# Three places in the instruction order of a two-layer decoder trunk: one copy, two loads and one step of gate arithmetic

## The chip, the core and the metric

The kernel runs on one core of a Trainium2 chip. The metric is the device time of one execution in microseconds (us), and of several runs their median. The core's engines work side by side, each through its own queue in order: TensorE (PE) multiplies matrices, with weight loads as a stream of their own (PEld); VectorE (DVE) and ScalarE (ACT) do elementwise work; SyncE (SP) issues the transfers (DMA) between HBM and the core's memory SBUF. PE writes its sums into PSUM, which here is a pool of eight banks. An engine that needs another's result waits for its semaphore, and everything behind it in its queue waits too.

## The reference, cut to what matters

Input x is 1024 tokens by 1024 numbers, float32. There are two layers, each a token mixer followed by an MLP, with an RMSNorm ahead of each, residual adds, and one RMSNorm at the end.

```
layer 0:  x = x + dilated_attention(rmsnorm(x))       # 3 groups of 8 heads, merged
          x = x + (relu(h @ w_up)**2) @ w_down         # MLP, 1024 -> 4096 -> 1024
layer 1:  q, k, v, g_out, gate_lr = split(h @ w_in)    # gated linear attention, 4 heads
          log_a = log_sigmoid(gate_lr @ w_gate_up + b) / 16
          o = chunked recurrence over (q, k, v, log_a), chunks of 64
          x = x + (rmsnorm(o) * silu(g_out)) @ w_out
          x = x + MLP as above
out = rmsnorm(x)
```

## The kernel before

**Products.** Every float32 operand is split into a rounded high part (made on ACT) and the remainder (made on DVE), and each product is three matmuls: high by high, high by low, low by high. The large products are Strassen-like: seven products (q or s = 0 to 6) of half-size blocks instead of eight, whose sums are formed by ACT copies and DVE adds out of PSUM.

**The first half of each MLP** (class Up, run at L668). It goes through 16 column blocks p, each with seven products s of 12 matmuls (L596). Product s of block p accumulates into bank "XYXVXZV"[s], so bank X takes s = 0, 2 and 4 in turn, and its contents are copied out (L601, tile e) after each of these before the next may write: e1, e2, e3. From p = 4 on (L703) the program issues in each step s: the product, then what `done(p, s - 1)` says of the product before, then `stage(p + 1, s)`, one piece of the weights for the next block (rounding on ACT, L533, remainder on DVE, L534, differences t on DVE, L561 to L571). At s = 2, done is the add c11 (DVE, L633) and its two squares, Relu and Square (ACT, L605 and L606), and a store; at s = 3, done is the copy e2. Product 4 must wait for e2. Rows p = 0 to 3 are written out by hand; p = 4 takes over from them.

**The gated layer's values and output gates** (gla_values, L1718; class Mixed, L872). 28 steps n, 24 matmuls each (L823), in two rounds g: steps 0 to 13 make g_out, steps 14 to 27 make v. Products accumulate into two sets of four banks, A and B. `sums(n)` (L845) copies finished banks on ACT (L890 or L833) and adds others on DVE (L838). `prep(n + 2)` splits the weights two steps ahead (ACT L802, DVE L808 and L778). The 16 finished pieces of g_out then go through the gate, one a step from n = 7 on, in three stages: `begin` (ACT exp, L902), in the next step `guard` (DVE, L907) and `logs` (ACT ln and exp, L912 and L913), in the one after `close` (three DVE instructions, L919 to L921, and a store to ggscr, L922). In step n the order is guard, close, sums, prep, load, product, logs, begin. From step 24 on `W.pump()` also prepares the next stage's weights (ACT L151, DVE L152).

**The heads** (gla_keys, L1935). For each of four heads h and two halves: `start_gates`, then `dense_T` for keys and for queries (24 matmuls each, L213 to L215). Between them, ticks run the previous head's recurrence: pairs of outputs are squared on ACT (L1823), scaled on DVE (L1830) and stored to oscr (L1835). In the last half of the last head, two loads of 512 KB each bring back finished outputs (ahead_k4, L1234, tiles ol), and during the query product `turn(0)` transposes them on PE (L259), which the output projection needs.

**What sets the order.** The order of each engine's queue is the order in which the program issues, written by hand. Tiles come from pools: k4 (25 buffers), t2 (8 buffers, among them c, e, gd, ge and gy), PSUM banks (8). A new tile waits for the last reader of the buffer that it gets. SP issues transfers in order, and a store waits there for its data.

## Time and profile before

| what | value |
|---|---|
| median of 3 runs | 2626.88 us (2626.61 to 2629.28) |
| the profiled execution | 2625.36 us |
| its span, first to last instruction | 2623.6 us |
| PE busy | 2588.1 us, 99% |
| DVE busy, ACT busy | 1860.3 us (71%), 1275.9 us (49%) |
| DMA, share of the 16 engines | 50.3% |
| mean granted clock of PE | 0.999 |

A row of a timeline has the start in us, the time taken in us, the engine, the line, the operation with its output and inputs, and how many were merged (x2). In square brackets stands the idle time of the engine before it and who ended it. A row of the list of waits has the waiting engine and line, what it waited for, and the total, the number and the longest in us. Line numbers are those of the kernel before.

### The profile page before, as it was taken

The page shows a single profiled execution, that of the slowest core. Times are in us where ns is not written, and L with a number is a line of the kernel's source. Part 1 is how long each engine was busy: PE and PEld are TensorE (multiplying, and loading weights), DVE is VectorE, ACT ScalarE, POOL GpSimd, SP SyncE. Part 2 cuts the span into 40 slices and gives each one's busy share as a digit, 9 for nine tenths or more (in the row PEclk, how much of TensorE's full clock was granted, in tenths as well). Part 3 has the DMA queues.
Part 4 walks back from the last instruction along what each step waited for, and adds up shares of the span by engine and source line. Part 5 has one row for each costly group of instructions (what it writes and reads, how often), then busy time and mean ns, then how long its engine had stood idle before and what let it go on. Part 6 is the DMA issues. An engine that isn't in the chain of part 4 may idle for free.

```text
span 2623.6 us, 33036 instructions
## 1 busy us (share of the span) xinstructions
PE 2588.1 (99%) x12144; PEld 2159.7 (82%) x12144; DVE 1860.3 (71%) x2986; ACT 1275.9 (49%) x2319; POOL 1.8 (0%) x7
## 2 busy tenths in 40 slices
PE   8999999999999999999999999999999999999998
PEld 6888888888888888888888887878888888888887
DVE  7645888888888768666657577977658866656666
ACT  6333455556555446555533345654326555553343
POOL 0000000000000000000000000000000000000000
PEclk9999999999999999999999999999999999999999
DMA  5533365655656633454775452462513545395543
GB/s 189 168 129 125 101 162 137 158 155 144 159 144 182 221 121 129 165 169 138 284 249 185 137 191 93 142 188 97 190 55 127 171 141 169 123 353 206 186 147 125
DMA packets 327010, 423.12 MB, mean 161 GB/s; under 512 B 19808, under 2 KB 192224, under 8 KB 326848
## 3 DMA queue, kind: packets, MB, share of 16 engines
q1 hardware_dynamic: 326848, 421.01, 50.3%
q8 instruction: 95, 1.56, 0.2%
q14 instruction: 67, 0.55, 0.1%
HBM read 279.71 MB, written 116.06 MB: 151 GB/s over the span
## 4 chain that ended last, share of the span: by engine, by line
PE 87%; DVE 7%; ACT 2%; issue 1%; DMA 1%; SPq 0%; ACTq 0%; DVEq 0%
PE pX L596 16%; PE pB L1570 13%; PE pV L596 10%; PE pA L1570 10%; PE pB L823 6%; PE pY L596 5%; PE pZ L596 5%; PE pA L823 5%; PE pd L214 3%; PE pd L215 3%; PE pd L213 3%; PE pS L970 2%; PE pO L1011 2%; PE pP L997 1%; PE pT L332 1%
## 5 line engine op out<-in xcount | busy, mean ns | idle before, releaser
L1570 PE MATMUL pB<-dh 128*128 128x512 f32 x512 | 199.7, 390 | 0.0
L1570 PE MATMUL pB<-dh,dl 128*128 128x512 f32 x512 | 199.5, 390 | 0.0
L1570 PE MATMUL pB<-dl,dh 128*128 128x512 f32 x512 | 199.5, 390 | 0.0
L222 DVE TENSOR_TENSOR dl<-sin,dh 128x1024 fp32r<-128x1024 f32 x112 | 136.7, 1220 | 44.8 <-ACT dh L219 44.2
L219 ACT ACTIVATE dh<-sin 128x1024 fp32r<-128x1024 f32 x112 | 117.9, 1052 | 90.1 <-PE pB L1570 32.6
L219 ACT ACTIVATE dh<-kept 128x1024 fp32r<-128x1024 f32 x64 | 67.9, 1061 | 183.6 <-DVE kept L1535 137.8
L596 PE MATMUL pV<-s4h,wd 128*128 128x512 f32 x448 | 151.0, 399 | 0.0
L1570 PE MATMUL pA<-dh 128*128 128x512 f32 x384 | 149.6, 390 | 0.0
L1570 PE MATMUL pA<-dl,dh 128*128 128x512 f32 x384 | 149.6, 390 | 0.0
L1570 PE MATMUL pA<-dh,dl 128*128 128x512 f32 x384 | 149.6, 390 | 0.0
L986 ACT ACTIVATE pt<-pt,orow 128x128 f32<-128x128 f32 (+1 forms) x192 | 84.7, 442 | 95.0 <-DVE orow L984 95.0
L1570 PEld LDWEIGHTS pB<-dh,dl 128*128 128x128 f32 x512 | 96.2, 188 | 19.9
L1570 PEld LDWEIGHTS pB<-dh 128*128 128x128 f32 x512 | 96.2, 188 | 19.8
L1570 PEld LDWEIGHTS pB<-dl,dh 128*128 128x128 f32 x512 | 96.2, 188 | 19.8
L534 DVE TENSOR_TENSOR wal<-raw,wah 128x512 fp32r<-128x512 f32 x112 | 76.2, 687 | 42.7 <-ACT wah L533 42.7
L605 ACT ACTIVATE c<-c 128x512 f32<-128x512 f32 x64 | 40.4, 631 | 125.0 <-DVE c L633 81.2
L596 PEld LDWEIGHTS pV<-s4h,wd 128*128 128x128 f32 x448 | 84.2, 188 | 17.6 <-DVE rb L621 0.3
L534 DVE TENSOR_TENSOR wbl<-t,wbh 128x1024 fp32r<-128x1024 f32 x56 | 68.6, 1226 | 39.0 <-ACT wbh L533 39.0
L222 DVE TENSOR_TENSOR dl<-kept,dh 128x1024 fp32r<-128x1024 f32 x64 | 78.4, 1225 | 24.9 <-ACT dh L219 19.0
L984 DVE CUSTOM_DVE_ANT_0 pt<-pS,masks 128x128 f32<-128x128 f32 (+1 forms) x192 | 58.3, 348 | 52.1 <-PE pS L970 52.1
L596 PE MATMUL pX<-s3h,wgh 128*128 128x512 f32 x224 | 87.8, 392 | 2.3 <-ACT e L601 2.3
L596 PE MATMUL pY<-a12h,wah 128*128 128x512 f32 x224 | 89.6, 400 | 0.0
(336 smaller groups left out, 7374.4 us busy)
## 6 DMA issues: line engine op xcount, KB each, us to landing
sin<-acts SPq DMA_DIRECT2D x112, 512.0 KB, 3.7
raw<-in_mlp_w_up_dram SPq DMA_DIRECT2D x64, 512.0 KB, 5.9
acts<-s SPq DMA_DIRECT2D x64, 512.0 KB, 3.4
raw<-in_mlp_w_down_dram SPq DMA_DIRECT2D x64, 512.0 KB, 4.6
raw<-in_attn_w_in_dram SPq DMA_DIRECT2D x96, 256.0 KB, 4.3
cw<-c SPq DMA_DIRECT2D x192, 128.0 KB, 2.3
acts<-c SPq DMA_DIRECT2D x64, 256.0 KB, 2.2
kept<-in_mlp_w_down_dram SPq DMA_DIRECT2D x32, 512.0 KB, 5.7
```

Source lines behind the costliest of these rows:

```text
L213: pe.matmul(ps, sh, mh, start=start, stop=False)
L214: pe.matmul(ps, sh, ml, start=False, stop=False)
L215: pe.matmul(ps, sl, mh, start=False, stop=stop)
L219: act.activation(hi, src, AF.Copy)
L222: dve.tensor_tensor(lo, src, hi.bitcast(F32), op=OP.subtract)
L534: self.remain(lambda: dve.tensor_tensor(lo, src, hi.bitcast(F32), op=OP.subtract))
L596: pe.matmul(st[b], u[:, k, :], v, start=first and k + n == 0, stop=k == 3 and n == 2, skip_group_check=True)
L823: pe.matmul(self.acc[s][t], a[:, c], b[:, k, :], start=fresh and m + k + v == 0, stop=m == 1 and k == 1 and v == 2, skip_group_check=True)
L970: pe.matmul(ps[:, i, :128 * n], self.qT[:, 128 * b:128 * b + 128], self.kT[:, k0:k0 + 128 * n], start=True, stop=True)
L984: dve.tensor_tensor_reduce(pt[:, i, :128 * n], ps[:, i, :128 * n], masks[:, m0:m0 + 128 * n], -scale, 1e38, op0=OP.add, op1=OP.min, accum_ ...
L986: act.activation(pt[:, i, :128 * n], pt[:, i, :128 * n], AF.Exp, scale=-1.0, bias=m, accum_out=self.row[:, r, HD:HD + 1])
L1570: pe.matmul(self.acc[s][t], a[:, k, c], b[:, k, :], start=fresh and m + k + v == 0, stop=m == 7 and k == 1 and v == 2, skip_group_check=True)
```

## The change

Three edits, each to the order in which work is issued. No instruction is added or taken away, and PE's queue is the same as before.

1. In the first half of both MLPs, at p = 4: the two squares of c11 and their store move from step 2 to step 3, behind the copy e2. The add c11 stays. On ACT's queue the order "square, square, copy" becomes "copy, square, square"; nothing else moves.
2. In the gated values, step 13 leaves out guard, close, logs and begin. The ten pieces that begin at step 13 or later run one step later. On DVE, four instructions leave step 13, a guard comes into step 24 and the last close into step 25 (between the wlo of the next stage's weights and the adds of that step); on ACT an exp comes into step 23 and ln and exp into step 24; on SP the last store to ggscr comes behind four loads of the next stage's weights.
3. In the last half of the last head, the two loads ol are issued ahead of the key product instead of behind it. On SP they stand behind one store to oscr of that stretch instead of three.

```
@@ Up.run
                     if s == 1:
                         self.sums(p - 1)
                         self.load(p + 2)
-                    if s > 0 and (p, s) != (4, 1):
+                    if (p, s) == (4, 2):
+                        self.add(4, 1)
+                    elif s > 0 and (p, s) != (4, 1):
                         self.done(p, s - 1)
+                    if (p, s) == (4, 3):
+                        self.squared(4, 1)
                     self.stage(p + 1, s)
@@ gla_values
         for n in range(4, m.STEPS):
-            m.guard()
-            m.close()
+            if n != 13:
+                m.guard()
+                m.close()
             m.sums(n)
...
-            m.logs()
-            if n >= 7:
-                m.begin()
+            if n != 13:
+                m.logs()
+                if n >= 7:
+                    m.begin()
             if n + 3 < m.STEPS:
@@ gla_keys
             start_gates(2 * h + half + 1)
+            if h == GH - 1 and half:
+                ol.extend(ahead_k4(p) for p in range(2))
             dense_T(w[0], hT, half, k_done)
             if h == GH - 1 and half:
-                ol.extend(ahead_k4(p) for p in range(2))
                 turn1.append(Turned(ol, xscr))
             dense_T(w[1], hT, half, q_done, half and (lambda: [t.turn(0) for t in turn1]))
```

## The prediction

> **What bounds the kernel now.** I read the page first, then the list of what TensorE (PE) waits for, then the timelines of PE, its weight loads (PEld), ACT, DVE and SP around each wait that an edit can reach.

> ```profile
> span 2623.6 us, 33036 instructions
> PE 2588.1 (99%) x12144; PEld 2159.7 (82%) x12144; DVE 1860.3 (71%) x2986; ACT 1275.9 (49%) x2319; POOL 1.8 (0%) x7
> PEclk9999999999999999999999999999999999999999
> ```

> PE is busy for 99% of the span, at the full granted clock throughout. No edit takes a matmul away, so only PE's idle time can be won: 2623.6 - 2588.1 = 35.5 us. In the list of PE's waits (total, times, longest, in us) four rows matter:

> ```profile
> PE pT L332 <- DVE xn L252: 11.9, 11, 9.2
> PE pX L596 <- ACT e L601: 2.3, 2, 1.1
> PE pT L259 <- DMA ol<-oscr: 2.0, 1, 2.0
> PE pB L823 <- DVE gq L838: 1.2, 1, 1.2
> ```

> The first is mostly the start of the kernel, which no edit touches. The other three, 5.5 us together, are one for each edit: two stops at the copy, one at the loads, one in the gates. The question is how much of each stays away.

> **Edit 1: the copy ahead of two squares, at p = 4 of both MLPs.** Rows of PE, ACT and DVE there, and the same copy one block later:

> ```profile
> 1060.40 0.39 PE L596 MATMUL pV<-s1h,wbl 128*128 128x512 f32 x1
> 1061.92 0.50 PE L596 MATMUL pX<-s3h,wgh 128*128 128x512 f32 x1 [1.13 <-ACT e L601]
> 1064.78 0.39 PE L596 MATMUL pZ<-a22h,wgh 128*128 128x512 f32 x1
> 2092.01 0.50 PE L596 MATMUL pX<-s3h,wgh 128*128 128x512 f32 x1 [1.13 <-ACT e L601]
> 1060.08 0.63 ACT L605 ACTIVATE c<-c 128x512 f32<-128x512 f32 x1 [2.51 <-DVE c L633]
> 1060.75 0.63 ACT L606 ACTIVATE c<-c 128x512 f32<-128x512 f32 x1
> 1061.29 0.58 ACT L601 ACTIVATE e<-pX 128x512 f32<-128x512 f32 x1
> 1061.76 1.05 ACT L533 ACTIVATE wbh<-t 128x1024 fp32r<-128x1024 f32 x1
> 1060.68 0.69 DVE L562 TENSOR_TENSOR t<-raw,t 128x512 f32<-128x512 f32 x1
> 1064.59 0.69 DVE L571 TENSOR_TENSOR t<-raw,t 128x512 f32<-128x512 f32 x1
> 1065.47 1.05 ACT L533 ACTIVATE wgh<-t 128x1024 fp32r<-128x1024 f32 x1
> 1079.97 0.58 ACT L601 ACTIVATE e<-pX 128x512 f32<-128x512 f32 x1
> 1080.87 0.19 PEld L596 LDWEIGHTS pX<-s3h,wgh 128*128 128x128 f32 x1
> 1670.81 0.39 PE L823 MATMUL pB<-dh,a12h 128*128 128x512 f32 x1
> 1671.94 0.39 PE L823 MATMUL pB<-dh,a12l 128*128 128x512 f32 x1
> ```

> The last two rows give the pace of PE: five steps in 1.13 us, 0.227 us a matmul (the bracket's idle time is taken from modelled ends, so I count starts). Without the stop, the first pX matmul would start at 1060.40 + 0.23 = 1060.63, and pZ twelve matmuls later at 1063.35. It starts at 1064.78: one stop costs 1.43 us. Its cause is plain: the two squares wait for DVE, and the copy, whose PSUM bank was complete when PE left product 2, stands behind them. Put ahead, it is done before PE asks. The squares lose nothing: they still start at 1060.08, when DVE has made c; so does the store behind them.

> What is late next? With the copy gone from there, ACT can round wbh when t (L562) is there, 1060.68 + 0.69 + 0.03 = 1061.40, which is 0.36 us sooner. DVE's next pieces follow wbh, so L571 ends at 1064.59 - 0.36 + 0.69 = 1064.92, and wgh starts at 1064.94 instead of 1065.47: 0.53 us sooner. From wgh to the copy of the next block I find ACT and DVE handing on to each other (wgl, rb, its squares, wd, c12, its squares, wah, the sums, c11, its squares), never waiting for PE. So that copy, still behind its squares at p = 5, moves from 1079.97 by 0.53 only and ends at 1079.44 + 0.58 = 1080.02. PE, 1.43 us ahead, wants the weight load of 1080.87 at 1079.44. It goes at about 1080.06: 0.81 us are kept of it, about 0.85 with the faster restart. After that the chain starts from PE's own pX again and is as far ahead as PE. **Kept: 0.85 us, twice: 1.7 us.** Bounds: nothing of it (0) and all of it (2.9); I take the value at which the rows arrive.

> **Edit 2: step 13 of the gated values without gate arithmetic.** Step 14's product waits at its third bank, which DVE's adds of step 13 must free; they stand behind a guard and three close instructions:

> ```profile
> 1673.52 0.50 PE L823 MATMUL pB<-dh,a12h 128*128 128x512 f32 x1 [1.19 <-DVE gq L838]
> 1683.22 0.39 PE L823 MATMUL pA<-dh,a11h 128*128 128x512 f32 x1
> 1670.38 0.43 DVE L907 TENSOR_SCALAR gd<-gd 128x512 f32<-128x512 f32 x1 [0.48 <-ACT gd L902]
> 1670.73 0.68 DVE L919 TENSOR_TENSOR gd<-gd,ge 128x512 f32<-128x512 f32 x1
> 1672.78 1.28 DVE L838 TENSOR_TENSOR gq<-pA,gq 128x512 f32<-128x512 f32 x2
> 1670.26 1.07 ACT L890 ACTIVATE gq<-pA 128x512 f32<-128x512 f32 x2
> 1671.21 1.06 ACT L802 ACTIVATE dh<-raw 128x1024 fp32r<-128x1024 f32 x1
> ```

> Product 14 has 48 matmuls up to the first pA: 1670.81 + 48 x 0.2267 = 1681.69, but pA starts at 1683.22. The stop costs 1.53 us. Without the four instructions the adds wait for ACT's two copies of the same banks only: the first is done near 1670.85, so the adds run from 1670.9 to 1672.1, and PE wants the bank at 1672.17. The stop goes.

> The ten items still to begin then run one step later, each with its exponentials on ACT and its store on SP. DVE's adds come 1.9 us sooner (1672.78 to 1670.9); its next instruction waits for the rounding that ACT ends at 1671.21 + 1.06 = 1672.27, which leaves 1.7. DVE has no idle time from there to step 24, so it stays 1.7 ahead. The bill comes at steps 24 and 25, where no gate work stood before: a guard (0.35) in 24, and three instructions (1672.78 - 1670.73 = 2.05 us) in 25, behind the wlo of the next stage and ahead of the adds that free two banks:

> ```profile
> 1734.29 1.06 ACT L151 ACTIVATE whi<-raw 128x1024 fp32r<-128x1024 f32 x1 [1.28 <-DMA raw<-in_gla_w_in_dram]
> 1735.38 1.23 DVE L152 TENSOR_TENSOR wlo<-raw,whi 128x1024 fp32r<-128x1024 f32 x1 [3.13 <-ACT whi L151]
> 1736.53 0.68 DVE L838 TENSOR_TENSOR c<-pB,c 128x512 f32<-128x512 f32 x1
> 1738.75 0.19 PEld L823 LDWEIGHTS pB<-dh,a22h 128*128 128x128 f32 x1
> ```

> That wlo waits for a load that SP issues behind stores of step 24, so it comes 1.7 - 0.35 = 1.35 us sooner, not 1.53. The first add then ends at 1736.53 + 0.68 - 1.35 + 2.05 = 1737.91, and PE wants it for the weight load of 1738.75 - 1.53 = 1737.22: a new stop of 0.69 us. **Kept: 1.53 - 0.69 = 0.84 us.** Bounds: -0.5 (the load comes no sooner at all, and the new stop is 2.05) and 1.53 (it comes 2.05 sooner, and there is none). I take the value by the stores, which tie the load to DVE. The store that is moved behind four loads on SP is read only by the load of gG in the heads, much later.

> **Edit 3: two loads ahead of a product.** SP, PE, ACT, the landing times of these loads, and DVE:

> ```profile
> 1868.25 14.73 SPq L1835 DMA_DIRECT2D oscr<-gy  x3
> 1883.07 0.96 SPq L1234 DMA_DIRECT2D ol<-oscr  x2
> 1884.72 0.40 PE L215 MATMUL pd<-a22h,wlo 128*128 128x512 f32 x1
> 1887.11 1.09 PE L259 MATMUL pT<-ident,ol 128*128 128x128 f32 x8 [1.99 <-DMA ol<-oscr]
> 1869.87 0.38 ACT L1823 ACTIVATE gy<-pO 128x256 f32<-128x256 f32 x1 [0.39 <-PE pO L1822]
> DMA to landing us min/median/max: 4.0/5.7/9.5
> 1885.51 0.88 DVE L1830 SCALAR_TENSOR_TENSOR gy<-pO,y,gG 128x256 f32<-128x256 f32 x2
> ```

> The transposes would start at 1884.95 and start at 1887.11: 2.16 us. The loads stood on SP behind three stores that wait one after another for DVE. Now they stand behind the first only, and go at 1868.7, or, if the buffer that they wait for is set free by the last ACT work ahead of them (the square at 1869.87), at 1870.3. Even by the longest landing, 9.5 us, they are there at 1879.8, before 1884.95. What is late next: the first rounding of the transposes stands on DVE behind gy, 1885.51 + 0.88 = 1886.4, about 0.1 late. The two stores are behind loads that are issued at once, so they lose nothing. **Kept: 2.1 us.** Bounds: 1.3 (all of gy's 0.88 shows) and 2.16.

> **Sum:** 1.7 + 0.84 + 2.1 = 4.64 us. The profiled execution took 2625.36 us (its span and 1.8 us around it): it becomes 2620.7. The median of the runs, 1.5 us longer, becomes 2626.88 - 4.64 = **2622.2 us**, with 2621.2 to 2623.2 as this case's own range.

> [...] From 1061.92 to 1064.78 twelve matmuls take 2.86 us, 0.238 each against 0.227. [...]

> **The rivals.**
> - Nothing is given back. If the chain at p = 5 has more slack than I count, and the load at step 24 lands sooner, the gain is 2 x 1.43 + 1.53 + 2.16 = 6.55 us: 2620.3. For it: the given-back pieces are sub-microsecond differences of long chains. Against it: the rows add up without a gap.
> - The clock falls at a stop. Twelve matmuls at half rate would take 5.44 instead of 2.86 us; four such stops would give 10 us more, 2612. Against it: the row of 1064.78.
> - Only the loads pay: both other stops come back one step later in full. Gain 2.1 us: 2624.8. Against it: the freed 0.53 and 1.35 us above.
> - Slower: the loads' wait for a buffer, now ahead of two stores on SP. If it were set free only after the third store's time, SP would hold the stores of gy, the squares would wait for a gy buffer, and pO on PE behind them. It decides from a release at 1880.9 on (plus 4.0 is 1884.95); past it each microsecond costs one, and past 1885.7, when the old stop of 2.16 and the other edits' 2.54 us are eaten up, the kernel is slower; a release at 1892 gives 2633. Against it: the ACT work ahead of the loads ends at 1870.3.

> **How the numbers follow.** 0.2% of 2626.88 is 5.25 us, about what a measurement of this kernel can tell from no change; the forecast lies just inside. Chances: forecast 0.50, of which 0.15 beyond 5.25 us by the scatter of the runs (2626.61 to 2629.28); nothing given back 0.33; clock 0.04; only the loads 0.06; slower 0.07. Faster: 0.15 + 0.33 + 0.04 = 0.52; within: 0.35 + 0.06 = 0.41; slower 0.07. The range leaves out the clock and the slower case and reaches from 0.7 us below the second case, for scatter, to just above the fourth: 2619.6 to 2625.2.

> **What would show it.** In the changed kernel's list of PE's waits, the rows for e (1.1 at p = 4), gq at step 14 and ol are gone. Right: two new small rows, pX for e at p = 5 of each MLP, and pB for c at step 26. If those are missing, the gain is near 6.5. Wrong: a wait for ol that is still there, a row of gy behind SP, or a matmul pace other than 0.227.

## The result, and the profile after

The changed kernel takes 2620.82 us, the median of 10 runs (2620.32 to 2621.96), against 2626.95 us for the kernel before (10 runs, 2625.72 to 2629.28): ratio 0.9977, 95% interval 0.9969 to 0.9985, which is 3.9 to 8.1 us. The medians are 6.1 us apart where the forecast had 4.64. The profiled executions are 4.2 us apart (2625.36 and 2621.12). Why these two differences differ is the main question of the experiments.

The page of the changed kernel, then its list of PE's waits and that of the weight loads' waits (in both: total, times, longest, in us):

```profile
span 2619.3 us, 33039 instructions
...
PE 2588.7 (99%) x12144; PEld 2159.3 (82%) x12144; DVE 1860.2 (71%) x2986; ACT 1276.5 (49%) x2319; POOL 1.8 (0%) x7
```

```profile
PE pT L332 <- DVE xn L252: 12.1, 11, 9.3
...
PE pB L827 <- DVE c L842: 0.2, 1, 0.2
```

```profile
PEld pX L596 <- ACT e L601: 1.7, 4, 0.5
...
PEld pB L827 <- DVE c L842: 0.6, 1, 0.6
```

Three rows of before are gone from PE's list: pX for e (2.3), pB for gq (1.2) and pT for ol (2.0). One that the forecast named has come, pB for c. The other, pX for e at p = 5, stands only in the list of the weight loads: four small waits, two in each MLP. (From here on, line numbers of the changed kernel are 4 to 7 higher than those of before.)

**Edit 1.** PE, weight loads and ACT around p = 4 and p = 5 of the first MLP, from the timelines:

```profile
1061.12 0.39 PE L596 MATMUL pV<-s1h,wbl 128*128 128x512 f32 x1
1061.35 0.39 PE L596 MATMUL pX<-s3h,wgh 128*128 128x512 f32 x1
...
1075.03 0.19 PEld L596 LDWEIGHTS pX<-s2h,wbh 128*128 128x128 f32 x1 [0.35 <-ACT e L601]
...
1080.83 0.19 PEld L596 LDWEIGHTS pX<-s3h,wgh 128*128 128x128 f32 x1 [0.48 <-ACT e L601]
...
1058.83 0.60 ACT L601 ACTIVATE e<-pX 128x512 f32<-128x512 f32 x1 [0.53 <-PE pX L596]
1060.81 0.63 ACT L605 ACTIVATE c<-c 128x512 f32<-128x512 f32 x1 [1.38 <-DVE c L633]
...
1079.66 0.63 ACT L606 ACTIVATE c<-c 128x512 f32<-128x512 f32 x1
1080.20 0.58 ACT L601 ACTIVATE e<-pX 128x512 f32<-128x512 f32 x1
```

At p = 4 the copy runs 2 us ahead of the squares, and pX follows pV by 0.23 us: no stop. At p = 5 the copy still stands behind the squares, and the weight load of 1080.83 waits for it, as forecast; another, at 1075.03, waits for e1, the first copy of that block, which stands behind other work of ACT and which the forecast did not name.

**Edit 2.** DVE and PE at steps 13, 14, 25 and 26:

```profile
1670.74 1.29 DVE L842 TENSOR_TENSOR gq<-pA,gq 128x512 f32<-128x512 f32 x2 [0.96 <-ACT gq L894]
...
1733.66 1.23 DVE L152 TENSOR_TENSOR wlo<-raw,whi 128x1024 fp32r<-128x1024 f32 x1 [2.80 <-ACT whi L151]
...
1736.86 1.28 DVE L842 TENSOR_TENSOR c<-pB,c 128x512 f32<-128x512 f32 x2
...
1670.64 0.39 PE L827 MATMUL pB<-dh,a12h 128*128 128x512 f32 x1
...
1681.53 0.39 PE L827 MATMUL pA<-dh,a11h 128*128 128x512 f32 x1
...
1737.60 0.50 PE L827 MATMUL pB<-dh,a22h 128*128 128x512 f32 x1 [0.15 <-DVE c L842]
```

The adds of step 13 wait for ACT alone and start at 1670.74; product 14 runs its 48 matmuls without a stop, 1670.64 + 48 x 0.227 = 1681.53. At step 25 wlo comes sooner, but the three instructions of the last close stand between it and the adds, and PE waits for these at 1737.60.

**Edit 3.** SP's queue and PE:

```profile
1866.94 0.36 SPq L1841 DMA_DIRECT2D oscr<-gy  x1
1867.40 0.97 SPq L1238 DMA_DIRECT2D ol<-oscr  x2
1872.36 13.12 SPq L1841 DMA_DIRECT2D oscr<-gy  x3
...
1883.43 0.39 PE L215 MATMUL pd<-a22h,wlo 128*128 128x512 f32 x1
1883.66 1.04 PE L259 MATMUL pT<-ident,ol 128*128 128x128 f32 x8
```

The loads go behind one store and hold up nothing; 16 us later the transposes follow the matmul before them without a stop.

**Where the time went, matmul by matmul.** PE's queue is the same in all kernels below (one has nine matmuls more), so the start of a matmul in one trace less the start of the same matmul in the first trace of before gives a shift at each place. The table has the median shift of the matmuls in some stretches (us; minus is sooner; times are those of before). A step between two columns is what an edit did between them; the first column is what came before any edit.

| kernel | 1046 to 1060, ahead of all edits | 1065 to 1074, behind p = 4 | 1640 to 1670, ahead of step 14 | 1684 to 1700, behind it | 1754 to 1767, behind step 26 | 1873 to 1885, ahead of ol | 1896 to 1925, behind it | 2095 to 2103, MLP 2, p = 4 | 2118 to 2150 |
|---|---|---|---|---|---|---|---|---|---|
| the change | +0.72 | -0.71 | -0.16 | -1.69 | -1.23 | -1.30 | -3.45 | -4.84 | -4.26 |
| copy_only | +0.47 | -0.96 | -0.44 | -0.48 | -0.47 | -0.46 | +1.22 | -0.20 | +0.37 |
| pause_only | +0.33 | +0.33 | +0.33 | -1.19 | -0.59 | -0.65 | +1.24 | +1.26 | +1.26 |
| loads_only | +0.96 | +0.97 | +0.99 | +0.90 | +0.92 | +0.92 | -1.21 | -1.18 | -1.18 |
| loads_mid | -0.16 | -0.15 | -0.18 | -0.25 | -0.25 | -0.24 | -2.41 | -2.43 | -2.43 |
| loads_copy | +1.47 | +0.04 | +0.63 | +0.65 | +0.67 | +0.66 | -1.49 | -2.92 | -2.35 |
| copies_p5 | +0.65 | -0.78 | -0.79 | -2.31 | -1.65 | -1.71 | -3.86 | -5.27 | -5.27 |
| close_behind | +0.49 | -0.94 | -0.97 | -2.49 | -2.47 | -2.50 | -4.65 | -6.05 | -6.05 |
| before_again | +1.48 | +1.48 | +1.50 | +1.45 | +1.48 | +1.47 | +3.17 | +3.23 | +3.23 |
| wait_covered | +1.31 | +1.30 | +1.26 | +1.29 | +1.31 | +1.31 | +1.48 | +1.48 | +1.48 |
| loads_swapped | +1.82 | +1.81 | +1.84 | +1.84 | +1.86 | +1.87 | +5.62 | +5.64 | +5.64 |

For the change: edit 1 takes 1.43 in MLP 1 and gives back 0.55, and 1.4 and 0.6 in MLP 2; edit 2 takes 1.53 and gives back 0.46; edit 3 takes 2.15. Together 4.98 us, less the 0.72 us that this execution was late ahead of all edits: the 4.26 of the last column.

### The profile page after: what moved, and what is told of

It is laid out like the page before. It is cut to its first block, busy times and chain, and to the rows that moved or that the text cites. A ratio compares the mean times of both kernels' runs of the same rounds, so it can differ in the third digit from the quotient of the medians.

```text
span 2619.3 us, 33039 instructions
## 1 busy us (share of the span) xinstructions
PE 2588.7 (99%) x12144; PEld 2159.3 (82%) x12144; DVE 1860.2 (71%) x2986; ACT 1276.5 (49%) x2319; POOL 1.8 (0%) x7
## 3 DMA queue, kind: packets, MB, share of 16 engines
q8 instruction: 95, 1.56, 0.2%
## 4 chain that ended last, share of the span: by engine, by line
PE 84%; DVE 10%; ACT 3%; issue 2%; DMA 1%; SPq 0%; ACTq 0%; DVEq 0%
PE pX L596 14%; PE pB L1574 13%; PE pA L1574 10%; PE pV L596 9%; PE pB L827 6%; PE pY L596 5%; PE pZ L596 5%; PE pA L827 4%; PE pd L214 3%; PE pd L215 3%; PE pd L213 3%; PE pO L1015 2%; PE pS L974 2%; PE pP L1001 1%; DVE dl L812 1%
## 5 line engine op out<-in xcount | busy, mean ns | idle before, releaser
L596 PE MATMUL pV<-s4h,wd 128*128 128x512 f32 x448 | 151.1, 399 | 0.0
L605 ACT ACTIVATE c<-c 128x512 f32<-128x512 f32 x64 | 40.4, 632 | 122.7 <-DVE c L633 79.0
L596 PEld LDWEIGHTS pV<-s4h,wd 128*128 128x128 f32 x448 | 84.3, 188 | 17.7 <-DVE rb L621 0.4
L596 PE MATMUL pY<-a12h,wah 128*128 128x512 f32 x224 | 89.6, 400 | 0.0
L596 PE MATMUL pZ<-a22h,wgh 128*128 128x512 f32 x224 | 89.4, 399 | 0.0
```

The lines of the kernel that those rows point to most:

```text
L596: pe.matmul(st[b], u[:, k, :], v, start=first and k + n == 0, stop=k == 3 and n == 2, skip_group_check=True)
```

## The experiments

Ten kernels ran. Medians are of 8 to 11 runs each (before_again is one run), beside a shared pool of runs of before (2627.0 to 2627.2 us in each call); intervals are those of the ratio.

**Each edit alone.**

*copy_only* has edit 1's hunk alone, *pause_only* edit 2's two, *loads_only* edit 3's.

> Edit 1 alone, the other two places as before. Theory (the forecast's step): each stop of 1.43 us at p = 4 goes and 0.85 of it stays, 1.7 us in all: about 2625.2 us, and the weight loads wait for e once at p = 5 of each MLP (0.3 to 0.5 us each). Rival (nothing given back): 2.9 us, 2624.1, no wait for e at p = 5. Second question, why the medians of before and after are 6.1 us apart and their two profiles only 4.3: if the landing time of the two loads ol differs from run to run and the profiled run of before had a short one, this kernel, which still waits for them, keeps the wide scatter of before (2625.7 to 2629.3), and is to be judged by its trace.

> Edit 2 alone. Theory: the stop of 1.53 us at step 14 goes, a stop of 0.2 to 0.7 us comes at step 26: gain 0.84 (forecast) to 1.1 us (the shift between the two traces already seen), about 2625.9 us. Rival (nothing given back): 1.5 us, and no wait at step 26. By the landing-time theory this kernel too keeps the scatter of before, over 3 us from lowest to highest.

> Edit 3 alone. Theory A (only the stop in the profile of before goes): gain 2.1 to 2.2 us, about 2624.8 us, and runs as scattered as those of before. Theory B (the loads' landing differs from run to run, and the profiled run of before had one of the shortest, 4.0 us): gain 3 to 4 us, about 2623.3 us, and runs within 1.7 us like those of after.

| kernel | median (lowest to highest), us | ratio | kept by the trace |
|---|---|---|---|
| copy_only | 2625.70 (2624.25 to 2627.06) | 0.9994 (0.9985 to 1.0002) | 1.43 - 0.52 and 1.42 - 0.57: 1.76 |
| pause_only | 2626.75 (2625.01 to 2629.54) | 0.9999 (0.9990 to 1.0008) | 1.52 - 0.60: 0.92 |
| loads_only | 2623.77 (2623.29 to 2624.77) | 0.9988 (0.9979 to 0.9996) | 2.13 |

By the traces, edits 1 and 2 give back about what the forecast said, and the rival "nothing given back" falls. The medians of the first two cannot carry such sizes: these kernels keep the scatter of before, 2.8 and 4.5 us, and loads_only has lost it (1.5). So the wait for ol has a part in it, and loads_only gains 3.2 us in the runs where its trace moves by 2.13. The table shows the rest from the other side: copy_only and pause_only, which keep the wait, lose 1.68 and 1.89 us at ol against the first trace of before. The reason is not only the landing time, as expected theory B had it. PE of copy_only behind the wait, and the granted clock in windows of copy_only and then of before, cut at whole steps of 3.413 us from a change of the clock in each (the last section has these steps; the columns are the stretch and its length; busy time and instructions of PE, PEld, DVE, ACT, POOL; granted clock of PE, share of the DMA engines, GB/s):

```profile
1884.26 0.40 PE L215 MATMUL pd<-a22h,wlo 128*128 128x512 f32 x1
1886.79 1.97 PE L259 MATMUL pT<-ident,ol 128*128 128x128 f32 x8 [2.14 <-DMA ol<-oscr]
...
1888.98 0.63 PE L214 MATMUL pd<-a22l,whi 128*128 128x512 f32 x1
1889.41 0.63 PE L215 MATMUL pd<-a22h,wlo 128*128 128x512 f32 x1
...
1890.19 0.40 PE L214 MATMUL pd<-a22l,whi 128*128 128x512 f32 x1
1890.43 0.40 PE L215 MATMUL pd<-a22h,wlo 128*128 128x512 f32 x1
```

```profile
1883.27:1886.68 3.41, 1.39 (x6) 0.77 (x5) 1.52 (x6) 0.89 (x3) 0.00 (x0) 1.00 1.00 294
1886.68:1890.09 3.41, 3.30 (x12) 3.01 (x13) 1.36 (x2) 1.89 (x3) 0.00 (x0) 0.50 1.02 299
```

```profile
1883.13:1886.54 3.41, 1.99 (x11) 1.38 (x9) 1.53 (x6) 0.89 (x3) 0.00 (x0) 1.00 0.80 259
1886.54:1889.95 3.41, 2.84 (x19) 2.53 (x20) 1.51 (x3) 2.14 (x4) 0.00 (x0) 1.00 1.00 327
```

Behind a wait of 2.14 us the eight transposes take 1.97 us instead of 1.09, and the next matmuls 0.43 us each (1888.98 to 1889.41) instead of 0.23 (1890.19 to 1890.43), for 3.41 us; the granted clock is 0.50 in that time. In the first trace of before, whose wait was 1.99 us, it is 1.00. In copy_only's step ahead of the fall, 1883.27 to 1886.68, PE was busy for 1.39 of 3.41 us and idle for 2.02; in the one of before, 1883.13 to 1886.54, it was busy for 1.99 and idle for 1.42.

**Edits 1 and 3 together.**

> Edits 1 and 3 together, to price edits 1 and 2 between kernels whose runs scatter little (edit 3 alone: 2623.77 us, 2623.3 to 2624.8). Theory: edit 1 is worth the 1.8 us by which its trace moves (0.97 in the first MLP, 0.87 in the second), so 2622.0 us, and edit 2 the rest to 2620.8, 1.1 to 1.2. Rival (the four medians of single edits as they stand): edit 1 1.25 us, 2622.5, and edit 2 0.2 alone.

2622.48 us (2620.95 to 2624.72), ratio 0.9983 (0.9975 to 0.9992). By medians edit 1 is worth 1.29 us and edit 2, against the change, 1.66; by the traces 1.70 (1.43 - 0.59 and 1.43 - 0.57) and 1.07. The median is the one that the rival expected (2622.5). But this kernel's runs scatter by 3.8 us, without the wait for ol, so the medians do not decide; the steps of the table do. What makes this kernel's runs differ was not tried; the table shows that executions differ by up to 2 us ahead of all edits (first column), but one trace of this kernel cannot show its runs.

**Both copies early at p = 5 too.** On top of the change:

```
-                    if (p, s) == (4, 2):
-                        self.add(4, 1)
-                    elif s > 0 and (p, s) != (4, 1):
+                    if p in (4, 5) and s == 2:
+                        self.add(p, 1)
+                    elif s > 0 and (p not in (4, 5) or s != 1):
                         self.done(p, s - 1)
-                    if (p, s) == (4, 3):
-                        self.squared(4, 1)
+                    if p in (4, 5) and s == 3:
+                        self.squared(p, 1)
```

and at s = 0 and 1 the copy e1 and c12's two squares change places for p = 5 as they have for p = 4.

> The changed kernel, and at p = 5 of each MLP the copy e1 ahead of c12's two squares and the copy e2 ahead of c11's, as at p = 4. Theory (what edit 1 gives back is the copies that stand behind their squares at p = 5): the four small waits of the weight loads for e go, 0.5 to 0.6 us per MLP: about 2619.7 us. Rival (ACT and DVE as a whole are late there, and the wait only moves to p = 6 or to the weights wbh and wgh): 2620.8 us as the changed kernel, with the waits in other rows.

2619.78 us (2619.20 to 2622.26). ACT and PE at p = 5:

```profile
1077.80 0.60 ACT L601 ACTIVATE e<-pX 128x512 f32<-128x512 f32 x1 [2.62 <-PE pX L596]
1078.29 0.62 ACT L605 ACTIVATE c<-c 128x512 f32<-128x512 f32 x1
```

```profile
1080.09 0.39 PE L596 MATMUL pV<-s1h,wbl 128*128 128x512 f32 x1
1080.32 0.39 PE L596 MATMUL pX<-s3h,wgh 128*128 128x512 f32 x1
```

The copy now waits for PE instead of the other way round, no weight load waits for e anywhere, and in the table nothing is given back: -0.78 stays -0.79, -5.27 stays -5.27. What edit 1 gives back is these two copies and nothing else.

**The last close behind the adds.** On top of copies_p5:

```
             if n != 13:
                 m.guard()
-                m.close()
+                if n != 25:
+                    m.close()
             m.sums(n)
+            if n == 25:
+                m.close()
```

> The kernel with both copies early also at p = 5, and besides the last close, at step 25, behind the adds of that step instead of ahead of them. Theory (what edit 2 gives back is the adds that stand behind that close): PE's wait for c at step 26 goes, 0.35 to 0.6 us, 2619.3 us. Rival (DVE is late as a whole): the wait comes back in another row, dl at step 27 or pA, and the time stays at 2619.8.

2620.00 us (2618.87 to 2620.81), by median no better than copies_p5: the runs do not show the gain that was expected. In the trace (DVE, step 25) the wait is gone and none has come:

```profile
1733.11 1.23 DVE L152 TENSOR_TENSOR wlo<-raw,whi 128x1024 fp32r<-128x1024 f32 x1 [2.67 <-ACT whi L151]
1734.26 1.28 DVE L842 TENSOR_TENSOR c<-pB,c 128x512 f32<-128x512 f32 x2
1735.45 0.68 DVE L923 TENSOR_TENSOR gd<-gd,ge 128x512 f32<-128x512 f32 x1
```

All of edit 2's gain stays (-0.97 to -2.49, and -2.47 behind step 26), 0.6 us more than copies_p5 keeps. This trace gains 6.54 us from its first column to its last, the most of all, and its span is 2617.5 us. It and copies_p5 are the best of these kernels, about 1 us under the change; the runs do not tell the two apart.

**The other order of the two loads, and the kernel before again.** In loads_swapped the one that PE asks for first is issued second:

```
-                ol.extend(ahead_k4(p) for p in range(2))
+                ol.extend([ahead_k4(p) for p in (1, 0)][::-1])
```

> The kernel before, with the two loads ol issued in the other order: the one that PE asks for first goes 0.48 us later and behind the other's 512 KB, so PE's stop for it grows from 2.0 to 2.5 to 3.5 us. Theory C (the clock of PE falls to half behind this stop in those executions in which the stop is long enough: two profiles with a stop of 2.1 and 2.2 us have granted clocks of 0.72 to 0.81 and 0.43 us a matmul behind it, the one of before, 2.0 us, has neither): the clock falls in nearly every execution, the time rises by the longer stop and by 1 us more, 2628 to 2629 us, and most runs have a mean clock of 0.998 or less. Theory D (the landing time alone makes the scatter): the time rises by the longer stop only, 0.5 to 1.5 us, and the granted clock in its profile is 1.00 behind the stop.

> The kernel before once more, unchanged, for a second profile of it. Theory C: by the 30 runs of before, 12 of which have a mean clock of 0.998 or less, the chance is about one half that the clock falls behind the stop at ol here; if it does, the profiled time is 1.5 to 2 us longer than the 2625.4 of the first profile, and if it does not, within 1 us of it. Theory D: the granted clock stays 1.00 and the time follows the landing time of ol alone.

loads_swapped: 2630.03 us (2629.13 to 2630.98), ratio 1.0013 (1.0004 to 1.0022). before_again: 2628.56 us, one run, 3.2 us above the first profile of the same kernel; 1.48 of these stood ahead of all edits (table). PE at the wait and the window behind it, in loads_swapped and in before_again:

```profile
1891.13 1.79 PE L259 MATMUL pT<-ident,ol 128*128 128x128 f32 x8 [4.13 <-DMA ol<-oscr]
```

```profile
1892.00:1896.00 4.00, 4.00 (x20) 3.45 (x19) 2.09 (x4) 3.57 (x5) 0.00 (x0) 0.65 0.96 331
```

```profile
1888.78 1.97 PE L259 MATMUL pT<-ident,ol 128*128 128x128 f32 x8 [2.19 <-DMA ol<-oscr]
```

```profile
1888.00:1892.00 4.00, 3.22 (x12) 2.94 (x13) 1.28 (x2) 1.82 (x3) 0.00 (x0) 0.57 1.04 307
```

The clock falls in both, and before_again is the same program as before: 1.47 to 3.17 in the table is 1.70 us at the wait, for 0.2 us more of waiting. In loads_swapped the wait grew by 2.1 us, more than I expected, and the table loses 3.8 there in all (1.87 to 5.64). The runs lie close together again, 1.9 us, as when each pays for the clock. One part of the expectation missed: only 5 of its 11 runs have a mean clock of 0.998 or less. Half a clock for 3.4 us is 0.0006 of the whole run, too little for a mean of three digits, so that means of a run tell nothing here; the windows do.

**The wait filled with work.** before, and on PE ahead of the waiting transposes:

```
+                if turn1:
+                    ps = bank("px")
+                    for _ in range(9):
+                        pe.matmul(ps, w[1][0][:, 0, :], hT[1][0].parts(0)[0], start=True, stop=True)
```

> The kernel before, with nine matmuls more on PE ahead of the transposes that wait for ol, into a bank that nobody reads (work beyond the reference's, 9 x 0.227 = 2.04 us). PE reaches the transposes when ol lands, so the wait itself is hardly changed, but PE is not idle in it. Theory C (idle PE loses its clock there, 1.6 us a time, in about three of four executions): granted clock 1.00 behind it, the idle time before the transposes at most 0.3 us, and although PE has 2 us more to do the median falls by 1.0 to 1.3 us, to about 2625.8. Theory D (the clock has no part in the gain of edit 3): the median stays within 0.3 us of before, 2627.0.

```profile
1886.26 2.22 PE L1975 MATMUL px<-a21h,whi 128*128 128x512 f32 x9
1888.62 1.06 PE L259 MATMUL pT<-ident,ol 128*128 128x128 f32 x8
```

```profile
1888.00:1892.00 4.00, 3.87 (x26) 3.14 (x25) 2.05 (x4) 2.71 (x4) 0.00 (x0) 1.00 0.94 268
```

With nine matmuls more the median is 2626.33 us (2625.03 to 2627.09), 0.84 under the 2627.17 of before in this call; the ratio's interval, 0.9988 to 1.0006, does not exclude no change, and it is less than the 1.0 to 1.3 us expected; but none of the 11 runs is above 2627.1, where 11 of the 21 runs of before are. Granted clock 1.00, and at the wait the table moves by 0.17 us instead of 1.7. So in these traces it was PE's idle time, not the wait for the data, that cost the 1.7 us.

**Half of edit 3.** The loads are issued in the middle of the key product, by a new argument of dense_T:

```
             if kt == 3:
                 tick()
+                if mid:
+                    mid()
...
-            dense_T(w[0], hT, half, k_done)
-            if h == GH - 1 and half:
-                ol.extend(ahead_k4(p) for p in range(2))
+            dense_T(w[0], hT, half, k_done, mid=h == GH - 1 and half and
+                    (lambda: ol.extend(ahead_k4(p) for p in range(2))))
```

> Edit 3 by half: the two loads in the middle of the key product, behind two of the three stores, ahead of the third alone. Forecast's working (the loads are early enough as long as they are issued before 1880.9; the second store goes at about 1873.7 us): no wait for ol, and the whole gain of edit 3 alone, 2623.8 us. Rival (the landing, up to 10 us, or the waiting store ahead of them makes them late): a wait for ol of up to 2 us remains, 2624.5 to 2627.

```profile
1868.00 5.78 SPq L1837 DMA_DIRECT2D oscr<-gy  x2
1873.87 0.96 SPq L1236 DMA_DIRECT2D ol<-oscr  x2
```

2624.06 us (2622.45 to 2624.93), ratio 0.9986 (0.9977 to 0.9995), no wait for ol, 2.17 us in the table: all of loads_only's gain. To have one store fewer ahead of the loads was enough.

## Why the prediction was right, and where it was short

- **Edit 1: right.** The stop was worth 1.43 us, as counted from the starts of matmuls, and 0.81 to 0.91 of it stayed in three kernels and both MLPs, where the forecast had 0.85. The give-back sits at p = 5 and nowhere else (copies_p5). It is two short waits, for e1 and e2, where the forecast had one of 0.81 for e2; and they show in the list of the weight loads, not, as announced, in PE's own.
- **Edit 2: right, a little short.** 1.53 us went, as forecast. The wait that came at step 26 cost 0.46 to 0.66 us in three traces, against 0.69; kept 0.86 to 1.07 against 0.84. The wlo that ties the new wait came sooner than counted: 1735.38 to 1733.66, of which PE's own lead was 0.16, so 1.56 us instead of 1.35, and that is the change's 0.46 instead of 0.69. close_behind shows that the last close ahead of the adds is the whole of it.
- **Edit 3: the wait right, its price too small.** 2.1 us were forecast and 2.13 to 2.17 measured in six traces. But in the runs edit 3 alone is worth 3.2 us. The forecast read its term from one execution, which happened to be one in which the clock stayed up. Missing was the 1.7 us that half-clock work behind the wait costs in part of the executions: 3 of 4 profiles with a wait of 2.0 to 2.25 us show it, and (3.18 - 2.13) / 1.7 gives an estimate of 0.6 of the runs. So the sum's premise, that only PE's idle time can be won, held for that one execution.
- **The clock rival, put at 0.04 and 10 us, was wrongly set aside.** The row that spoke against it (twelve matmuls at 0.238 us behind 1061.92) was right for a stop of 1.4 us, and in no trace here did the clock fall at the stops of edits 1 and 2 (1.43 and 1.53 us, granted clock 1.00 behind them). It was carried over to a stop of 2.0 us, for which it says nothing; and where the clock falls, it costs 1.7 us (half clock for 3.41 us) and not 2.6: no run shows the 10 us that the rival counted for four stops.
- **The sum.** By the traces of the single edits 1.76 + 0.92 + 2.13 = 4.81 us, and 4.98 by that of the change, against 4.64; with 1.05 for the clock 5.9 to 6.0, against 6.1 between the medians. What is left is within the scatter of before. The median of 2620.82 lies below the forecast's own range (2621.2 to 2623.2) and nearer to the rival "nothing given back" (2620.3): by the time alone one would have chosen that rival, although the traces show what edits 1 and 2 give back. The clock's term, which the sum did not have, hides it in the median.
- **Slower, by the loads' wait for a buffer:** did not happen; the stores behind the loads went as before.

Open: what makes executions differ by up to 2 us ahead of all edits. The shifts arise mostly in the first 25 us, at 728 us and from 850 to 870 us; the last two places lie in the attention, where PE waits for pt (0.89 us at 863 in the first trace of before, 1.07 in the change's) and e (0.46 us at 850 in wait_covered, 0.53 in loads_swapped), which ACT makes. In before_again a fall of the clock (last section) is among them; the cause of the others was not tried.

## What to carry to other kernels

When one stop is removed, find the next instruction that stands in the same order in its queue and ask by how much it moves: here that gave each give-back to within 0.3 us, and moving that next instruction too won it back. Compare traces by the shift of the same matmul, not by two totals: a stop of 0.5 us is plain there, and lost between medians that scatter by 3. Here the stop at ol, 2.0 to 2.2 us long, cost 1.7 us more than its length in 3 of 4 profiles, those in which the granted clock behind it was 0.50: one profile need not show such a cost; compare several.

## What the hardware showed that I had not expected

Behind a wait of 2.1 to 2.2 us (copy_only 2.14, before_again 2.19) the granted clock was 0.50 for 3.4 us (0.43 us a matmul instead of 0.227), at a price of 1.7 us; the same program with a wait of 1.99 us in another execution kept 1.00. Stops of 1.4 and 1.5 us left it at 1.00 in every trace here. Length alone is not it: in before_again the clock also fell in the attention, where PE is idle for 0.51, 1.07 and 0.16 us within 3 us:

```profile
861.99 0.94 PE L1011 MATMUL pO<-v,pt 128*128 128x128 f32 x6 [0.51 <-ACT pt L999]
864.00 0.33 PE L997 MATMUL pP<-ident,pt 128*128 128x128 f32 x1 [1.07 <-ACT pt L986]
864.49 0.69 PE L997 MATMUL pP<-ident,pt 128*128 128x128 f32 x2 [0.16 <-ACT pt L986]
...
866.74 0.63 PE L214 MATMUL pd<-wlo,oTh 128*128 128x512 f32 x1
867.16 0.63 PE L215 MATMUL pd<-whi,oTl 128*128 128x512 f32 x1
```

```profile
861.12:864.53 3.41, 1.67 (x12) 1.05 (x10) 3.35 (x11) 2.38 (x8) 0.00 (x0) 1.00 0.27 61
864.53:867.94 3.41, 3.41 (x12) 3.02 (x13) 3.38 (x7) 2.14 (x7) 0.00 (x0) 0.50 0.63 138
```

Here the fall came behind several short idle times, 1.74 us in all (1.67 of 3.41 us busy).

And a wait filled with nine matmuls that nobody needs moved the median down by 0.84 us, with an interval not clear of none, and not up.
